# All low halves of the streamed weights on VectorE in a two-layer mixer, none on GpSimd in attention and first merge

## The chip, the cores and the metric

The kernel runs on one core of a Trainium2 chip. The core has TensorE (PE in the profile: matmuls, with its weight loads as PEld), VectorE (DVE), ScalarE (ACT), GpSimd (POOL) and SyncE (SP, which here issues the DMAs). The metric is the device time of one execution in microseconds; less is better.

## The reference, cut to what matters

Two layers over 512 latent tokens and 256 context tokens of 1024 channels, in fp32. Each layer is a mixer of three branches with sigmoid gates, then an MLP with a squared ReLU. The context goes through the same weights; in the last layer only its keys and values are needed.

```python
for l in range(DEPTH):                                     # 2
    mod, mod_c = c_act @ w_ada[l] + b_ada[l], cc_act @ w_ada[l] + b_ada[l]
    h = modulate(rms_norm(x, norm1[l]), sh1, sc1)          # hc from xc in the same way
    (u, qs, ks_, vs, q1, q2, k1, k2, vd, gl) = project_streams(h @ w_in[l], ...)
    y_pool = pool_mixer(u, w_pool[l], pool_scale[l])
    y_swa = windowed_gqa_latent(qs, ks_, vs, ksc, vsc, swa_sink[l])
    y_diff = diff_head_out(diff_attention_latent(q1, q2, k1, k2, vd, ...), ...)
    merged = (g[..., 0, :] * (y_pool @ w_br_pool[l]) + g[..., 1, :] * (y_swa @ w_br_swa[l])
              + g[..., 2, :] * (y_diff @ w_br_diff[l]))    # g = sigmoid(gl)
    x = x + g1 * (merged @ w_out[l])
    h2 = modulate(rms_norm(x, norm2[l]), sh2, sc2)
    x = x + g2 * (jnp.square(jax.nn.relu(h2 @ w_ff1[l])) @ w_ff2[l])
    # layer 0: the same for the context xc
return x
```

## The kernel before

**Products in three parts.** Every fp32 operand of a large product is held as a high half H, its rounding to the matmul's fp32r type, and a low half L = operand - H. A product is hi*hi + hi*lo + lo*hi, three matmuls into one PSUM tile (L229 to L231 in `unit`, L376 in the projections, L988 to L990 in the gates).

**The stream of weights.** All weights of both layers lie in memory as one stream of tiles of 128 rows and up to 768 columns, in the order of their use. `dma_tile` loads the next tile into one of three raw buffers; all these loads are issued by SyncE in the order of the stream. `split_tile` takes the next raw tile, calls `split` and lets the next load go. `split` (L168) issues two instructions, both recorded at their own lines: ScalarE's copy to the high half (L170) and the subtraction that gives the low half (L171), on the engine `eng`, or on VectorE where `eng` is None. The result is a W tile, of which six exist (RING). `ensure` splits up to a given tile; `blocks` asks for the tiles of a unit and for some ahead of them.

**Who takes the low halves.** The tiles of the MLP and of the windowed groups are subtracted on VectorE. On GpSimd are those of the four differential groups (`group`), of the gates beside attention (`gate_filler`), of the gates and branches of the first layer's merge (the tables WG and WB, one entry for a layer), of half of the output projection (OUTE) and of some tiles of the prologue and of the first layer's MLP (PW, FE). Other work of GpSimd: the reciprocal roots (L178), a part of the rotary embedding (L439) and of its gains (L409, L413), halves of the y of two branches (YP, also L171, but with `y` as its output), and a part of the modulated activations h.

**The stages**, in us of the profiled execution: the prologue (to 60: first norm and modulation, first products); the first layer's attention (60 to 584: two windowed groups, four differential ones, where the projection of the next group and gates fill in between the softmax steps; the last part has the pooling branch as filler); the merge (584 to about 755: remaining gates, 24 branch products, each gated on VectorE at L1294 and L1298 and summed at L1301; beside it the modulation columns of later stages, dot products of VectorE with DMA'd rows of w_ada, L259); the output projection and the MLP (to 1340). The second layer repeats this from 1340 with less context work: attention 1400 to 1750, merge and output to 1925, MLP to the end.

**What sets the order.** Each engine works through its instructions in the order of the program. A list scheduler orders them by when their inputs are expected and by priorities (the table PRI, and `high_priority` ahead of L1294 and L1298); in the prologue the order is the one that is written. A split is thus placed where the scheduler thinks that its copy is done.

**Names**: W_nnn a W tile; E the exponentials of a softmax and PT their transposes (L702, L777, L592 scale E; L542, L719 take the low half of PT from PSUM); ob the output of attention, scaled; d, nm, rt, rc small columns of the softmax; x, xn, h activations and gs a gain; mg the merged branches, tgl a reloaded gate, br a branch product; junk the output of the dot products L259, of which only the sum counts.

Of the kernel before, what the change touches and what calls it, by code (L numbers as in the profile page):

```python
# [13 lines left out]
PSUM = bass.MemoryType.PSUM  # L14
# [13 lines left out]

# gates of the first branches that are worked out beside the attention of each group
GATES_AT = ((5, 5, 3, 3, 0, 1), (5, 5, 3, 3, 3, 1))  # L30
# [5 lines left out]
def unit_plan(l):  # L36
    """Each layer's weights in the order of their use: (name, index, tiles of 128 rows)."""
    g = START[l]
    seq = [("swa", 0, 0)] + [("gate", j, 8) for j in range(g)]
    for i, n in enumerate(GATES_AT[l]):  # L40
        if i < 5:
            seq.append(("swa", 1, 0) if i == 0 else ("diff", i - 1, 0))
        seq += [("gate", g + j, 8) for j in range(n)]
        g += n
    tail = [x for x in seq if x[0] == "gate"][g - GATES_AT[l][5]:]
    seq = [x for x in seq if x not in tail]
    seq += [("u", m, 8) for m in range(4)] + [("wp", 0, 4)] + tail
    seq += [(name, i, 8 if name == "gate" else 4) for name, i in merge_plan(l)]
    seq += [("out", m, 8) for m in range(8)] * 2
    return seq + [(name, i, 8 if name == "ff1" else 4) for name, i, _, _ in mlp_plan(l)]  # L50


def merge_plan(l):
    """Gates that are left after the attention, and the branches."""
    g = (START[l] + sum(GATES_AT[l]))
    first = min(24, max(g, 16) + AHEAD)
    seq = [("gate", i) for i in range(g, first)]
    for i in range(24):
        if i >= 16 and first < 24:
            seq.append(("gate", first))  # L60
            first += 1
        seq.append(("br", i))
    return seq


def mlp_plan(l):
    """The MLP by parts of 512 hidden channels: (name, unit, part, turn), the first units of a part before the
    second product of the last one. The last part of the first layer goes over the latents and then the context."""
    parts = [(e, 0) for e in range(8)] + ([(7, 1)] if l == 0 else [])
# [11 lines left out]
def stream_plan(seq):  # L81
    """Columns of each tile of the stream, and where each unit's row tiles lie in it."""
    tiles, where, room = [], {}, 0
# [31 lines left out]
MGP = ()  # L115
WG = ("pool", None)
WB = (("pool", "pool"), (None, None))
ATT = {"Q": 5, "E": 4, "PT": 3, "y": 2, "ph": 2, "zs": 3, "st": 6}
# [15 lines left out]
class Kern:  # L134
# [6 lines left out]

# [1 line left out]
    def T(self, name="T", dtype=F32):  # L143
# [17 lines left out]
    def psum(self, name, g, s):  # L161
        """The pool of the phase that begins: g single banks and s pairs of them."""
        if self.ps is not None:
# [9 lines left out]
    def rsqrt(self, out, in_, n, scale):  # L173
        """out = (in_*scale + eps) ** -0.5"""
        nc = self.nc
        t = self.sm(n, "ms")
        nc.vector.tensor_scalar(t, in_, scale, EPS, ALU.mult, ALU.add)  # L177
        nc.gpsimd.tensor_tensor(out, t, self.mhalf[:, 0:n], op=ALU.pow)  # L178

# [1 line left out]
    def dma_tile(self):  # L181
# [10 lines left out]
    def split_tile(self, eng=None):  # L192
        """Split the next tile of the weight stream into its two parts."""
        if self.pos >= len(TILES):
# [17 lines left out]
    def blocks(self, l, name, idx, ahead=2, eng=None, turn=0):  # L212
        """The row tiles of a unit's weights as (tile, column) pairs."""
        w = [(FIRST[l] + i, o) for i, o in STREAMS[l][1][name, idx][turn]]
        self.ensure(w[-1][0] + ahead, eng)
        return [(self.loaded[i], o) for i, o in w]

# [1 line left out]
    def unit(self, ps, W, acts, groups, off=0):  # L219
        """ps[:, tokens] = sum_k W_k^T acts_k as hi*hi + hi*lo + lo*hi."""  # L220
        mm = self.nc.tensor.matmul
# [10 lines left out]

# [1 line left out]
    def silu2(self, out, c, t):  # L234
        """2 * silu(c)"""
        self.nc.scalar.activation(t, c, AF.Tanh, scale=0.5)
# [18 lines left out]
    def ada_dot(self, pool, w, c, l, j):  # L255
        """Modulation column j as a product of rows; c holds twice the vector."""
        for v in range(2 if l == 0 or j < 16 else 1):
# [5 lines left out]
    def ada(self, raw, js):  # L263
        """Modulation columns, one of 128 channels at a time; the last layer's context needs only a norm."""
        pool, c = self.cvec(raw)
# [12 lines left out]

# [1 line left out]
    def norm_stats(self, x, a, b):  # L280
        """The tokens' 1/rms on every partition, in PSUM."""
        nc = self.nc
# [21 lines left out]
    def gains(self, l, v, j0, norm0):  # L304
        """gain * (1 + scale), for a norm whose scale starts at modulation column j0."""
        gs = self.cp.tile([128, 8], F32, name=f"gs{l}_{v}_{j0}")
# [9 lines left out]
    def modulate(self, t, h, k, a, b, gs, sh):  # L316
        """h = t * gain + shift in two parts; t is overwritten."""
        nc = self.nc
# [5 lines left out]
    def norm_apply(self, x, a, b):  # L324
        """x / rms in place."""
        bc = self.norm_stats(x, a, b)
# [12 lines left out]

# [1 line left out]
    def group(self, l, kind, gi):  # L341
# [3 lines left out]
        else:  # L345
            d = self.group_w(l, kind, gi, self.nc.gpsimd if kind == "diff" else None)
        if d["swa"]:
# [9 lines left out]
    def group_w(self, l, kind, gi, eng):  # L357
        """The weights and the shape of a group."""
        return dict(kind=kind, gi=gi, Q={}, swa=kind == "swa", dims=(4, 1, 64) if kind == "swa" else (2, 2, 128), done=set(),
                    W=[t for t, _ in self.blocks(l, kind, gi, 0, eng)])  # L360

    def proj_mm(self, l, h, d, t, k0, k1):
        """Half of the projection of token tile t."""
        st = d.setdefault(t, {})
# [127 lines left out]

# [1 line left out]
    def diff_unit(self, l, d, qt):  # L494
# [76 lines left out]
    def diff_ctx(self, l, d):  # L571
        """The two context query tiles of one head, over the context keys."""
        nc = self.nc
# [73 lines left out]

# [1 line left out]
    def swa_unit(self, l, d, qt, hp):  # L649
# [90 lines left out]
    def swa_ctx(self, l, d, qt):  # L740
        """One context query tile of four heads, over the context keys."""
        nc = self.nc
# [66 lines left out]

# [1 line left out]
    def attention(self, l, h, tail):  # L811
# [81 lines left out]
    def gate_filler(self, l, h, first, last):  # L893
        """Gates in half units, kept in memory until the merge."""
        nc = self.nc
        for i in range(first, last):
            W = self.blocks(l, "gate", i, 0, nc.gpsimd)
            for (a, b) in ((0, 384), (384, 768)) if l == 0 else ((0, 256), (256, 512)):
# [8 lines left out]

# [1 line left out]
    def kv(self, shape, name, dtype=F32):  # L909
        return self.kp.tile(shape, dtype, tag="KV", name=name)  # L910

    def pool_branch(self, l, h, groups):
        """u, the pooled means and their mixing; in steps, beside other work."""
        nc = self.nc
# [86 lines left out]

# [1 line left out]
    def prologue(self, pl):  # L1003
        """The first layer's norm, modulation and first products, in the order that is written here."""
        nc, a = self.nc, self.a
# [143 lines left out]
    def small(self, rows, P):  # L1149
        """Sinks, gains, lambdas and the scale of the heads' outputs."""  # L1150
        nc = self.nc
# [19 lines left out]

# [1 line left out]
    def run(self):  # L1173
# [48 lines left out]
        for l in range(DEPTH):  # L1222
# [12 lines left out]

            # attention
            if l > 0:
# [13 lines left out]

            # branches and merge
            pb = tc.tile_pool(name=f"pb{l}", bufs=1, reuse_waits="tile")
# [59 lines left out]

            # output projection, residual, MLP
            pm = tc.tile_pool(name=f"pm{l}", bufs=1, reuse_waits="tile")
# [111 lines left out]
def host_arrays(inp):  # L1427
# [59 lines left out]
    rows = np.concatenate(rows + [np.zeros(3 * 512 - DEPTH * ROWS_L, np.float32)]).reshape(3, 512)  # L1487
    # constants of the shapes alone
    f32 = np.float32
# [45 lines left out]
```

## Time and profile before

| | us |
|---|---|
| median of three runs (lowest to highest) | 2308.11 (2307.55 to 2310.36) |
| span of the profiled execution | 2309.9 |
| TensorE busy | 2212.6 (96%) |
| VectorE busy | 1502.7 (65%) |
| ScalarE busy | 962.3 (42%) |
| GpSimd busy | 520.8 (23%) |

The page gives the busy time of each engine; TensorE's share says how much of the span could go at most without fewer or faster matmuls. The stretches (windows) give the same by stage. A group of instructions of one line shows their count, mean duration and what the engine waited for ahead of them; the view of one line gives the least, median and greatest duration, which tells whether an instruction always takes the same time. The timeline lists single instructions with start and duration, and in brackets how long the engine stood idle ahead of one and for whom. The list of TensorE's waits sums these brackets.

### The profile page before, as it was taken

The numbers are of one execution on the slowest core, as the hardware profiler recorded it, in microseconds if no ns is written. First come the engines' busy times: TensorE is split into PE (matmuls) and PEld (weight loads), VectorE is DVE, ScalarE is ACT, GpSimd is POOL, SyncE is SP. The second block draws the span as 40 slices with busy tenths as digits, with TensorE's granted clock in tenths as the row PEclk, the third lists the DMA queues.
The fourth block names the chain that finished last, engine by engine and source line by source line (L and its number), as shares of the span: only waits on it lengthen the run. The fifth ranks groups of instructions, "written<-read, shape, count | busy, mean of one in ns | idle before, by whom it ended". The sixth has DMA issues, their size and how long they took to land.

```text
span 2309.9 us, 34112 instructions
## 1 busy us (share of the span) xinstructions
PE 2212.6 (96%) x12924; PEld 1969.0 (85%) x12924; DVE 1502.7 (65%) x2757; ACT 962.3 (42%) x1979; POOL 520.8 (23%) x525
## 2 busy tenths in 40 slices
PE   7999999989988999999999989999999999999999
PEld 2999999988876888888888879999998788888887
DVE  6667676777799776655555487766668577544443
ACT  4466655565212442222222244655556435332331
POOL 4334245432442200000000033434551122000000
PEclk9999999999998999999999989999999999999999
DMA  6222122212774543333333342212222654333332
GB/s 256 84 56 79 53 74 77 68 36 84 254 255 152 188 121 126 121 129 124 127 125 105 89 132 70 75 56 83 74 74 82 203 186 130 105 95 96 94 96 76
DMA packets 108668, 260.53 MB, mean 113 GB/s; under 512 B 13012, under 2 KB 33620, under 8 KB 107223
## 3 DMA queue, kind: packets, MB, share of 16 engines
q1 hardware_dynamic: 108502, 258.35, 35.2%
q8 instruction: 102, 1.67, 0.3%
q14 instruction: 64, 0.52, 0.1%
HBM read 233.00 MB, written 25.30 MB: 112 GB/s over the span
## 4 chain that ended last, share of the span: by engine, by line
PE 47%; issue 26%; DVE 15%; DMA 4%; ACT 4%; POOL 3%; SPq 0%; POOLq 0%; DVEq 0%; ACTq 0%
PE z L376 7%; PE ff L231 5%; PE ff L230 5%; PE ff L229 5%; PE gate L988 3%; PE gate L990 3%; PE gate L989 3%; DMA raw<-in_w_dram 2%; DMA wada<-in_wada_dram 2%; POOL W L171 2%; DVE junk L259 2%; DVE W L171 1%; ACT W L170 1%; PE ptr L715 1%; PE ada L1047 1%
## 5 line engine op out<-in xcount | busy, mean ns | idle before, releaser
L170 ACT ACTIVATE W<-raw 128x768 fp32r<-128x768 f32 (+1 forms) x383 | 320.2, 838 | 576.7 <-PE ff L231 428.2
L171 DVE TENSOR_TENSOR W<-raw,W 128x768 fp32r<-128x768 f32 x243 | 236.4, 974 | 189.4 <-ACT W L170 183.5
L376 PE MATMUL z<-W,h 128*128 128x384 f32 (+2 forms) x1728 | 313.5, 332 | 10.5 <-POOL h L1077 4.3
L171 POOL TENSOR_TENSOR W<-raw,W 128x768 fp32r<-128x768 f32 (+1 forms) x140 | 267.7, 1920 | 203.2 <-ACT W L170 199.3
L376 PEld LDWEIGHTS z<-W,h 128*128 128x128 f32 x1728 | 286.8, 191 | 14.6 <-POOL h L1077 5.1
L229 PE MATMUL ff<-h,W 128*128 128x512 f32 (+1 forms) x800 | 280.6, 351 | 1.2 <-ACT r L1350 1.2
L230 PE MATMUL ff<-h,W 128*128 128x512 f32 (+1 forms) x800 | 280.8, 351 | 0.0
L231 PE MATMUL ff<-h,W 128*128 128x512 f32 (+1 forms) x800 | 280.1, 350 | 0.0
L178 POOL TENSOR_TENSOR rs<-ms,mhalf 128x4 f32<-128x4 f32 (+4 forms) x79 | 79.7, 1009 | 867.2 <-DVE ms L177 829.0
L230 PE MATMUL ff<-f,W 128*128 128x512 f32 x736 | 264.2, 359 | 0.1
L229 PE MATMUL ff<-f,W 128*128 128x512 f32 x736 | 263.2, 358 | 0.0
L231 PE MATMUL ff<-f,W 128*128 128x512 f32 x736 | 262.4, 357 | 0.0
L259 DVE CUSTOM_DVE_ANT_0 junk<-wada,cbc,cols 128x1024 bf16<-128x1024 f32 x128 | 188.1, 1469 | 55.2 <-DMA wada<-in_wada_dram 54.4
L988 PE MATMUL gate<-h,W 128*128 128x256 f32 (+1 forms) x656 | 215.3, 328 | 6.4 <-DVE ob L554 6.4
L989 PE MATMUL gate<-h,W 128*128 128x256 f32 (+1 forms) x656 | 215.6, 329 | 0.0
L990 PE MATMUL gate<-h,W 128*128 128x256 f32 (+1 forms) x656 | 212.4, 324 | 0.0
L1380 DVE SCALAR_TENSOR_TENSOR x<-ff,mod,x 128x512 f32<-128x512 f32 (+1 forms) x192 | 121.4, 657 | 105.0 <-PE ff L231 104.8
L229 PEld LDWEIGHTS ff<-h,W 128*128 128x128 f32 x800 | 151.3, 189 | 22.9 <-ACT r L1350 1.4
L231 PEld LDWEIGHTS ff<-h,W 128*128 128x128 f32 x800 | 151.1, 189 | 21.6
L230 PEld LDWEIGHTS ff<-h,W 128*128 128x128 f32 x800 | 151.2, 189 | 21.4
L229 PEld LDWEIGHTS ff<-f,W 128*128 128x128 f32 x736 | 138.7, 189 | 21.7
L231 PEld LDWEIGHTS ff<-f,W 128*128 128x128 f32 x736 | 138.3, 188 | 21.3
(263 smaller groups left out, 4721.6 us busy)
## 6 DMA issues: line engine op xcount, KB each, us to landing
raw<-in_w_dram SPq DMA_DIRECT2D x375, 384.0 KB, 3.1
wada<-in_wada_dram SPq DMA_DIRECT2D x80, 512.0 KB, 4.1
wa<-in_wada_dram SPq DMA_DIRECT2D x8, 1024.0 KB, 8.1
tgd<-tgs SPq DMA_DIRECT2D x38, 192.0 KB, 2.3
tgl<-tgd SPq DMA_DIRECT2D x19, 384.0 KB, 4.5
tgd<-tgs SPq DMA_DIRECT2D x44, 128.0 KB, 1.9
tgl<-tgd SPq DMA_DIRECT2D x22, 256.0 KB, 4.2
yl<-yd SPq DMA_DIRECT2D x12, 384.0 KB, 3.9
```

The lines of the kernel that those rows point to most:

```text
L170: nc.scalar.activation(H, src, AF.Copy)
L171: (eng or nc.vector).tensor_tensor(L, src, H.bitcast(F32), op=ALU.subtract)
L178: nc.gpsimd.tensor_tensor(out, t, self.mhalf[:, 0:n], op=ALU.pow)
L229: mm(ps[:, a:b], wh, x[0][:, r], start=k == 0, stop=False)
L230: mm(ps[:, a:b], wh, x[1][:, r], start=False, stop=False)
L231: self.last_mm = mm(ps[:, a:b], wl, x[0][:, r], start=False, stop=k == nk - 1)
L259: self.nc.vector.tensor_tensor_reduce(junk, w, c[:, v, :], 0.5, self.col(l, 21 + j), ALU.mult, ALU.add, self.mod[l][:, v, j:j + 1])
L376: self.nc.tensor.matmul(z[:, c0:384], h[k][:, hpart, ts], d["W"][k // 2][:, wpart, (k % 2) * 384 + c0:(k % 2 + 1) * 384], start=(k == 0 an ...
L988: mm(ps, wh, x[:, 0, a:b], start=k == 0, stop=False)
L989: mm(ps, wh, x[:, 1, a:b], start=False, stop=False)
L990: return mm(ps, wl, x[:, 0, a:b], start=False, stop=k == len(acts) - 1)
L1380: nc.vector.scalar_tensor_tensor(x[m][:, ga:gb], ps[:, ga:gb], self.mod[l][:, v, 40 + m:41 + m], x[m][:, ga:gb], ALU.mult, ALU.add)
```

## The change

Four arguments change; each named GpSimd for a low half of W and now names none, which means VectorE. ScalarE's copies, the loads and their order, the ring and all numbers stay. (The other lines of the full diff only blank comments.)

```diff
@@ tables of the module
-WG = ("pool", None)
-WB = (("pool", "pool"), (None, None))
+WG = (None, None)
+WB = ((None, None), (None, None))
@@ group
-            d = self.group_w(l, kind, gi, self.nc.gpsimd if kind == "diff" else None)
+            d = self.group_w(l, kind, gi, None)
@@ gate_filler
-            W = self.blocks(l, "gate", i, 0, nc.gpsimd)
+            W = self.blocks(l, "gate", i, 0, None)
```

`blocks` also splits the tiles ahead of a unit on the engine named for it, so at the borders a tile of a neighbouring unit moves too. In the built program GpSimd has 140 subtractions of W before and 30 after, VectorE 243 and 353.

GpSimd, end of the prologue. x, h: the parts of the first activations that GpSimd modulates, the numbers 169 and 170 two of their buffers.

```order
 L171 TENSOR_TENSOR W_396<-raw,W_396 128x768
 L171 TENSOR_TENSOR W_401<-raw,W_401 128x768
-L171 TENSOR_TENSOR W_579<-raw,W_579 128x768
 L1074 TENSOR_SCALAR x_3_157<-x_3_157,gs_1_8_172,mod_124 128x256
 L1077 TENSOR_TENSOR h_169<-x_3_157,h_169 128x256
 L1074 TENSOR_SCALAR x_3_157<-x_3_157,gs_1_8_172,mod_124 128x256
 L1077 TENSOR_TENSOR h_170<-x_3_157,h_170 128x256
-L171 TENSOR_TENSOR W_584<-raw,W_584 128x768
```

Two splits are gone from GpSimd; the first stood ahead of the last two tiles of h, the second behind them. In VectorE's row they stand ahead of gs and behind its last h.

VectorE, first layer's attention, at about 185 to 190 us: the softmax of one query tile of a windowed group, whose scaled E (L702) TensorE transposes next.

```order
 L678 ISA nm 128x1
 L686 TENSOR_TENSOR d<-nm,nsink 128x2
+L171 TENSOR_TENSOR W_2243<-raw,W_2243 128x768
 L693 TENSOR_TENSOR rt<-r,es 128x2
 L695 RECIPROCAL rc<-rt 128x2
 L702 TENSOR_SCALAR E<-E,rc 128x512
+L171 TENSOR_TENSOR W_2248<-raw,W_2248 128x768
 L434 TENSOR_TENSOR xn<-zs,rg 128x320
 L732 TENSOR_TENSOR y<-O,ob 64x256
```

Two splits came into the row: one between the softmax's columns d and rt, one behind L702.

VectorE, the merge of the first layer: dot products of the modulation beside the gated branches.

```order
 L259 ISA junk,mod_124<-wada,cbc,cols 128x1024
 L259 ISA mod_124 128x1
+L171 TENSOR_TENSOR W_7205<-raw,W_7205 128x768
+L171 TENSOR_TENSOR W_7280<-raw,W_7280 128x768
 L1294 SCALAR_TENSOR_TENSOR mg<-tgl,br 128x768
 L259 ISA junk,mod_124<-wada,cbc,cols 128x1024
```

Two splits came in ahead of the first gated branch (L1294); the dot products keep their places around it.

## Rows read from the trace of the kernel before

**Rows 1.** The page, part 1: busy us, share of the span, instructions.

```profile
PE 2212.6 (96%) x12924; PEld 1969.0 (85%) x12924; DVE 1502.7 (65%) x2757; ACT 962.3 (42%) x1979; POOL 520.8 (23%) x525
```

**Rows 2.** Stretches: window, length, busy us of each engine (instructions), PEclk, DMA share, GB/s.

```profile
60.00:460.00 400.00, 390.62 (x2459) 380.36 (x2459) 267.20 (x646) 229.20 (x588) 152.42 (x165) 0.99 0.24 69
622.00:715.00 93.00, 80.30 (x434) 68.78 (x433) 90.40 (x109) 15.72 (x19) 32.66 (x15) 0.96 0.69 234
```

**Rows 3.** Groups, GpSimd, 60 to 460 us: busy us, mean ns, idle before.

```profile
L171 POOL TENSOR_TENSOR W<-raw,W 128x768 fp32r<-128x768 f32 x37 | 70.4, 1910 | 23.5 <-ACT W L170 23.4
```

**Rows 4.** Line L171, W: min/median/max ns, first and last start, forms.

```profile
L171 DVE TENSOR_TENSOR W<-raw,W x243: 694/958/2181, 89.3 to 2283.3; 128x768 fp32r<-128x768 f32 x121, 128x512 fp32r<-128x512 f32 x1
...
L171 POOL TENSOR_TENSOR W<-raw,W x140: 919/1846/2844, 38.0 to 1911.8; 128x768 fp32r<-128x768 f32 x133, 128x512 fp32r<-128x512 f32 x6, 128x256 fp32r<-128x256 f32 x1
```

**Rows 5.** Four other lines of VectorE, the same columns.

```profile
L702 DVE TENSOR_SCALAR E<-E,rc x32: 486/553/2052, 126.3 to 1578.4; 128x512 f32<-128x512 f32 x16, 128x640 f32<-128x640 f32 x16
L719 DVE TENSOR_TENSOR PT<-ptr,PT x80: 408/691/693, 130.7 to 1585.0; 128x512 fp32r<-128x512 f32 x64, 128x256 fp32r<-128x256 f32 x16
L259 DVE CUSTOM_DVE_ANT_0 junk<-wada,cbc,cols x128: 1271/1284/2926, 589.5 to 1244.6; 128x1024 bf16<-128x1024 f32 x128
L1301 DVE TENSOR_TENSOR mg<-mg,tgl x25: 677/947/2597, 663.1 to 1887.6; 128x512 f32<-128x512 f32 x14, 128x768 f32<-128x768 f32 x11
```

**Rows 6.** Timeline, first layer's attention: start us, us, engine, line.

```profile
187.51 1.84 POOL L171 TENSOR_TENSOR W<-raw,W 128x768 fp32r<-128x768 f32 x1
...
187.80 1.83 DVE L702 TENSOR_SCALAR E<-E,rc 128x512 f32<-128x512 f32 x1
```

**Rows 7.** Timeline, first layer's merge.

```profile
639.64 1.93 POOL L171 TENSOR_TENSOR W<-raw,W 128x768 fp32r<-128x768 f32 x1 [2.16 <-ACT W L170]
639.93 2.72 DVE L259 CUSTOM_DVE_ANT_0 junk<-wada,cbc,cols 128x1024 bf16<-128x1024 f32 x1
```

**Rows 8.** Groups by form, VectorE and GpSimd, merge, 584 to 715 us.

```profile
L259 DVE CUSTOM_DVE_ANT_0 junk<-wada,cbc,cols 128x1024 bf16<-128x1024 f32 x47 | 80.2, 1706 | 5.7 <-DMA wada<-in_wada_dram 5.1
L1301 DVE TENSOR_TENSOR mg<-mg,tgl 128x768 f32<-128x768 f32 x9 | 15.1, 1680 | 0.0
L171 POOL TENSOR_TENSOR W<-raw,W 128x768 fp32r<-128x768 f32 x18 | 41.5, 2308 | 52.8 <-ACT W L170 52.8
L171 POOL TENSOR_TENSOR y<-yl,y 128x768 fp32r<-128x768 f32 x6 | 13.3, 2217 | 25.5 <-ACT y L170 19.0 <-DMA wada<-in_wada_dram 6.5
```

**Rows 9.** What TensorE waits for, 60 to 460 us: total us, times, longest.

```profile
PE tr L473 <- DVE d L763: 2.2, 1, 2.2
PE ptr L715 <- DVE E L702: 1.4, 2, 0.7
PE tr L473 <- ACT E L592: 1.4, 1, 1.4
```

**Rows 10.** The same, second layer's attention, 1400 to 1750 us.

```profile
PE gate L988 <- DVE ob L554: 3.7, 2, 1.8
PE ptr L715 <- DVE E L702: 2.4, 2, 1.5
...
PE O L550 <- DVE PT L542: 1.4, 2, 0.8
```

**Rows 11.** The same, merge, 584 to 715 us.

```profile
PE br L229 <- DVE mg L1294: 6.2, 2, 3.3
```

**Rows 12.** Timeline, end of the prologue.

```profile
49.59 5.56 POOL L171 TENSOR_TENSOR W<-raw,W 128x768 fp32r<-128x768 f32 x3
...
57.59 2.68 PE L376 MATMUL z<-W,h 128*128 128x384 f32 x6 [4.31 <-POOL h L1077]
```

**Rows 13.** Timeline, start of the second layer.

```profile
1370.78 2.54 POOL L171 TENSOR_TENSOR W<-raw,W 128x768 fp32r<-128x768 f32 x1
...
1371.96 2.18 DVE L171 TENSOR_TENSOR W<-raw,W 128x768 fp32r<-128x768 f32 x1
...
1374.19 1.65 PE L376 MATMUL z<-W,h 128*128 128x384 f32 x4 [1.17 <-DVE W L171]
```

## What the change will do to the time: the prediction

> **What bounds the kernel now.** I read the share of each engine first. The reader should see that TensorE is busy 96% of the span and that nothing else is near: VectorE 65%, GpSimd 23% [rows 1]. A change on VectorE and GpSimd can therefore only take away, or add to, the few microseconds in which TensorE stands still. Next the stretches: in the long stretch of the first layer's attention (60 to 460 us) VectorE is busy 267 of 400 us, in the merge it is busy 90.4 of 93 us, which is 97% [rows 2]. So attention has room on VectorE and the merge has none. Then the two forms of the instruction that moves: a 128x768 low half has a median of 0.958 us on VectorE and 1.846 us on GpSimd [rows 4].
>
> The view that decides is the spread of the other VectorE instructions. L702 takes 0.486 us at best and 2.052 at worst, L259 1.271 and 2.926, L1301 0.677 and 2.597, while L719, which reads PSUM, never exceeds 0.693 [rows 5]. The timeline shows what the long ones have in common. An L702 starts at 187.80 and ends at 189.63; a GpSimd split started at 187.51 and ended at 189.35 [rows 6]. An L259 starts at 639.93 and takes 2.72; a GpSimd split ran until 641.57, and 641.57 plus an undisturbed 1.28 is 642.85, about where the L259 ends [rows 7]. I read this as: a VectorE instruction with its inputs in SBUF stands still until the GpSimd split that began before it is through. So the splits on GpSimd are not free for VectorE, and the question is whether VectorE loses more by doing them or by waiting for them.
>
> **What moves.** The order of the built program shows 110 splits gone from GpSimd's row (140 before, 30 after) and 110 more in VectorE's (243, then 353). By place: 2 in the prologue, 45 in the first layer's attention, 18 in its merge, 2 at the second layer's start, 43 in its attention. Six are of 512 columns at 0.694, 104 of 768 at 0.958: 6 x 0.694 + 104 x 0.958 = 103.8 us of new VectorE work. GpSimd loses some 205 us (110 x about 1.87; in the long stretch 37 of them were 70.4 us [rows 3]). None of this is on TensorE by itself: in the list of what TensorE waits for there is hardly a W outside the second layer's start, since the ring of six W tiles keeps them ready before use. That a single split becomes 0.9 us shorter is therefore costed at nothing; the ring hides it. What counts is what happens to VectorE's other instructions, stage by stage.
>
> **Merge of the first layer (584 to 715 us).** Removed: the standing still. 47 L259 at a mean of 1.706 against 1.284 undisturbed are 19.8 us too long, 9 L1301 at 1.680 against 0.947 are 6.6 us too long [rows 5, 8], 26.4 together. GpSimd ran 41.5 us of W splits and 13.3 us of y splits, which stay [rows 8]; the share of W is 41.5 / 54.8 = 76%, so 20.0 us go. Added: 18 x 0.958 = 17.2 us. Net on VectorE: -2.8. As VectorE is full there, and TensorE waits for its mg (6.2 us in two waits [rows 11]), the net goes to the end nearly whole. I take **-3**, with bounds of 0 (TensorE's waits have another cause) and -5 (the y halves that run beside are freed too).
>
> **Attention of both layers.** Added: 45 and 43 splits, 88 in all: about 41 us of VectorE work in each layer. Removed: held instructions. Pairing each VectorE instruction of two SBUF inputs (or one tensor_scalar) that exceeds its usual time with the split running beside it gives about 30 us a layer. Net some +10 us of VectorE work a layer in stretches with 130 us of free time, so throughput there is not the matter; single waits of TensorE are. From the lists of waits [rows 9, 10]:
> - E L702, 1.4 + 2.4 = 3.8 us in four waits. Each follows a held L702, as at 187.80. The hold was about 1.3 us, longer than the 0.7 waited there. I take -3.3.
> - d L763, 2.2 us. Two GpSimd splits stand beside the VectorE chain that leads to it. The splits come onto VectorE as 2 x 0.96, less than the 2 holds. I take -1.7.
> - E L592 1.4, PT L542 1.4, ob L554 3.7: 6.5 us where the held instruction stands further up the chain. I take a little under half, -2.9.
>
> Together **-7.9**; bounds 0 (each time the next wait comes up) and about -11.
>
> **Second layer's start.** A VectorE split of W took 2.18 us because a GpSimd split from 1370.78 to 1373.32 held it, and TensorE waited 1.17 us for it [rows 13]. With both on VectorE, the second stands behind the first, so the first takes 0.96: 2.18 - 0.96 = 1.22 us. **-1.2**.
>
> **Prologue.** GpSimd ran three W splits from 49.59 to 55.15, and TensorE then waited 4.31 us for GpSimd's h [rows 12]. The third of these goes to VectorE, so GpSimd's x and h start a third of 5.56, some 1.9 us, earlier. On VectorE it costs 0.96 ahead of gs, which delays ScalarE's part, but that part is done long before GpSimd's. **-1.9**; bounds 0 and -1.9.
>
> **Allowance.** 88 splits now stand in VectorE's row ahead of instructions that TensorE may wait for. When a copy by ScalarE ends late, VectorE's row stops. I allow **+2** (bounds 0 and +8).
>
> Sum: -3 - 7.9 - 1.2 - 1.9 + 2 = **-12**. The profiled execution's span is 2309.9, 1.8 above the median of the runs, 2308.1; from the span I get 2297.9, and with the same distance between the two **2296** for the median.
>
> **The rivals.**
> 1. *The waits only change their name.* TensorE's waits in attention are short and each has a next one close behind; if nothing of the 7.9 comes and half of the rest, the gain is about 3 us: 2305. For it: TensorE idles only about 9 of 400 us in the long stretch. Against it: the gains of merge and prologue don't rest on that.
> 2. *VectorE's row stops for ScalarE's copy: slower.* A split needs ScalarE's copy of the same tile, which waits for the tile's DMA. GpSimd's 37 splits of the long stretch waited 23.4 us for that copy, 0.63 us each [rows 3]. On GpSimd this hurt nobody; on VectorE the softmax of the group stands behind it. If two splits at each of the 12 starts of groups make TensorE wait, it costs 12 x 2 x 0.63 = 15 us, and the attention's -7.9 is lost: 2308 - 6 + 15 = 2317. It decides from 0.14 us of TensorE's time per moved split (88 x 0.14 = 12 eats the gain). Against it: the order puts each split where its copy is planned to be done.
> 3. *The merge is the bound: slower.* If the long L259 came from the traffic of the DMAs and not from GpSimd, VectorE would get 17.2 us more in a stretch that is 97% full and nothing back: 2308 + 17.2 - 7.9 - 1.2 - 1.9 + 2 = 2316. It decides once less than 17.2 - 9.0 = 8.2 of the 26.4 us goes, a third. Against it: L259 of 1.28 us and of 2.7 us stand side by side in the same traffic.
> The Trainium skill ("Perfetto Trace Analysis", section "Optimizing Scalar/DVE Operations") says that where DVE is saturated, giving some work to ScalarE or GpSimd may make sense; this change does the contrary in a saturated stretch, and by that rule alone the rival of 2316 would win. The same section adds that DVE and GpSimd share a read port of SBUF, so that moving work between those two might not help, and the held L259 agrees with the second sentence rather than the first (2.72 against 1.28 us).
> 4. *More goes than I counted.* If all that the splits hold turns into shorter chains (the 400 - 390.6 = 9.4 us that TensorE stands still in the long stretch [rows 2], as much in the second layer's attention, the merge's 6.2 and the 3.1 of the two starts), the gain is near 28: 2280.
> 5. *The change doesn't do what it says*: excluded by the order of the built program, which shows the 110 moved.
>
> **How the numbers follow.** Forecast (2289 to 2303) 0.67; more 0.05; waits change their name 0.15; slower by the row of VectorE 0.07; slower by the merge 0.06. About 0.2% (4.6 us) is what a measurement of this kernel can tell from no change, so faster means under 2303.5: 0.67 + 0.05 = 0.72; same 0.15; slower 0.13. The range leaves out the slower cases and most of the larger gain: 2284 to 2309.
>
> **What would show it.** If the steps are right: GpSimd's busy time falls by about 205 us and VectorE's grows by about 20 (103.8 added, 20 of holds in the merge and some 60 in the attentions removed); in 622 to 715 the mean L259 falls from 1.706 to about 1.35, not to 1.284, as y splits remain; L702 keeps near 0.5; the waits on E L702 and d L763 are gone; TensorE's wait for h in the prologue falls from 4.31 to about 2.4. If L259 stays at 1.7, rival 3 holds and the step on standing still is wrong. If TensorE has new waits whose releaser is a PT, E or Q of VectorE with a W split just ahead in its row, rival 2 holds. If VectorE grows by 100 us, the holds had another cause.

## The result and the profile after

The changed kernel takes 2275.2 us (median of four runs, 2274.2 to 2276.4) against 2308.5 before: a ratio of 0.986 with a 95% interval of 0.9848 to 0.9872, 33 us faster. The forecast was 2296 with a range of 2284 to 2309: the sign came out right, the forecast gain of 12 is about a third of what came, and the time lies below the range.

The page of the changed kernel, part 1 (busy us, share, instructions; it answers to [rows 1]), and the stretches that answer to [rows 2], with the second layer's attention, whose row in the kernel before stands in the third block (window, length, busy us of PE, PEld, DVE, ACT, POOL, granted clock, DMA share, GB/s):

```profile
PE 2202.3 (97%) x12924; PEld 1963.7 (86%) x12924; DVE 1517.3 (67%) x2867; ACT 963.5 (42%) x1979; POOL 324.9 (14%) x415
```
```profile
60.00:446.00 386.00, 385.18 (x2454) 376.57 (x2454) 272.29 (x683) 228.96 (x586) 84.98 (x125) 1.00 0.23 72
608.00:691.00 83.00, 78.65 (x438) 68.29 (x437) 80.36 (x111) 15.92 (x20) 7.18 (x3) 0.98 0.74 255
...
1373.00:1714.00 341.00, 338.17 (x2564) 333.49 (x2563) 249.05 (x628) 205.78 (x522) 81.99 (x134) 1.00 0.24 75
```
```profile
1400.00:1750.00 350.00, 340.25 (x2565) 333.44 (x2564) 239.66 (x583) 204.69 (x522) 154.90 (x177) 1.00 0.25 73
```

VectorE took over 110 splits and grew by 1517.3 - 1502.7 = 14.6 us, not by the 103.8 of their own time: the rest came back from instructions that no longer stand still. GpSimd lost 196 us. In the long stretch of the first attention TensorE stood still 400 - 390.6 = 9.4 us before and 386 - 385.2 = 0.8 after, and its busy time for nearly the same matmuls fell by 5.4 as well. In the second layer's attention it was 9.8 before and 2.8 after.

The durations, line by line (min/median/max in ns, first and last start), which answer to [rows 5], and the groups of the merge, which answer to [rows 8]:

```profile
L702 DVE TENSOR_SCALAR E<-E,rc x32: 471/517/555, 123.7 to 1547.1; 128x512 f32<-128x512 f32 x16, 128x640 f32<-128x640 f32 x16
L259 DVE CUSTOM_DVE_ANT_0 junk<-wada,cbc,cols x128: 1269/1280/2871, 574.6 to 1220.3; 128x1024 bf16<-128x1024 f32 x128
```
```profile
L259 DVE CUSTOM_DVE_ANT_0 junk<-wada,cbc,cols 128x1024 bf16<-128x1024 f32 x45 | 60.9, 1352 | 5.9 <-DMA wada<-in_wada_dram 5.6
L171 DVE TENSOR_TENSOR W<-raw,W 128x768 fp32r<-128x768 f32 x17 | 19.4, 1146 | 0.0
L1301 DVE TENSOR_TENSOR mg<-mg,tgl 128x768 f32<-128x768 f32 x10 | 9.5, 954 | 0.0
...
L171 DVE TENSOR_TENSOR y<-yl,y 128x768 fp32r<-128x768 f32 x6 | 7.3, 1225 | 0.0
```

L702 never exceeds 0.555 us now (2.052 before). L259 still reaches 2.87, beside the y splits and the output projection's W splits that stay on GpSimd. What TensorE waits for in the long stretch, in the merge, and in the second layer's attention (answers to [rows 9 to 11]; total us, times, longest):

```profile
PE tr L473 <- DVE rot L462: 0.7, 1, 0.7
PE z L376 <- ACT zs L395: 0.2, 1, 0.2
```
```profile
PE br L230 <- DVE y L171: 4.3, 1, 4.3
```
```profile
PE gate L988 <- DVE ob L554: 1.3, 2, 0.6
PE ptr L715 <- DVE Q L489: 0.8, 1, 0.8
```

The waits on E, d, PT and mg that the forecast had named are all gone, and most of ob. To see where the time went I laid the two traces side by side: each TensorE instruction of the one against the same of the other, and the difference of their starts at the borders of the stages.

| stage (us of before) | forecast | by the two traces |
|---|---|---|
| prologue, to 95 | -1.9 | +0.3 |
| first attention, 95 to 584 | some -3.6 | -13.7 |
| merge and output, 584 to 820 | -3 | -10 |
| MLP, and start of the second layer to 1400 | -1.2 | -3.5 |
| second attention, 1400 to 1750 | some -4.3 | -8.9 |
| the rest | 0 | -1.7 |
| allowance | +2 | |
| sum | -12 | -37.4 |

The sum of the traces is their spans' difference, 2309.9 - 2272.5; the span of the profiled execution lies 2.7 us below the median time for the changed kernel and 1.4 above it for the one before, which leaves 33 for the medians.

### The profile page after: what moved, and what is told of

Read it like the earlier page. It is cut to its first block, busy times and chain, and to the rows that moved or that the text cites. A ratio compares the mean times of both kernels' runs of the same rounds, so it can differ in the third digit from the quotient of the medians.

```text
span 2272.5 us, 34132 instructions
## 1 busy us (share of the span) xinstructions
PE 2202.3 (97%) x12924; PEld 1963.7 (86%) x12924; DVE 1517.3 (67%) x2867; ACT 963.5 (42%) x1979; POOL 324.9 (14%) x415
## 4 chain that ended last, share of the span: by engine, by line
PE 50%; issue 26%; DVE 14%; DMA 4%; ACT 3%; POOL 2%; SPq 0%; DVEq 0%; ACTq 0%; POOLq 0%
PE z L376 9%; PE ff L231 5%; PE ff L230 5%; PE ff L229 5%; PE gate L988 4%; PE gate L989 4%; PE gate L990 4%; DVE junk L259 2%; DVE W L171 2%; DMA raw<-in_w_dram 2%; PE ptr L715 1%; DVE nm L513 1%; DMA wada<-in_wada_dram 1%; PE ada L1047 1%; PE br L230 1%
## 5 line engine op out<-in xcount | busy, mean ns | idle before, releaser
L171 DVE TENSOR_TENSOR W<-raw,W 128x768 fp32r<-128x768 f32 (+1 forms) x353 | 346.8, 984 | 224.0 <-ACT W L170 219.6
L259 DVE CUSTOM_DVE_ANT_0 junk<-wada,cbc,cols 128x1024 bf16<-128x1024 f32 x128 | 173.9, 1359 | 52.1 <-DMA wada<-in_wada_dram 51.6
L229 PEld LDWEIGHTS ff<-f,W 128*128 128x128 f32 x736 | 138.8, 189 | 21.7
L231 PEld LDWEIGHTS ff<-f,W 128*128 128x128 f32 x736 | 138.3, 188 | 21.3
L230 PEld LDWEIGHTS ff<-f,W 128*128 128x128 f32 x736 | 138.6, 188 | 20.8 <-DVE f L1353 0.5
```

The lines of the kernel that those rows point to most:

```text
L171: (eng or nc.vector).tensor_tensor(L, src, H.bitcast(F32), op=ALU.subtract)
L229: mm(ps[:, a:b], wh, x[0][:, r], start=k == 0, stop=False)
L230: mm(ps[:, a:b], wh, x[1][:, r], start=False, stop=False)
L231: self.last_mm = mm(ps[:, a:b], wl, x[0][:, r], start=False, stop=k == nk - 1)
L259: self.nc.vector.tensor_tensor_reduce(junk, w, c[:, v, :], 0.5, self.col(l, 21 + j), ALU.mult, ALU.add, self.mod[l][:, v, j:j + 1])
```

## The experiments

**Each stage alone.** e1 has the two edits in attention, e2 the two tables of the merge.

```diff
 e1 (against the changed kernel)
-WG = (None, None)
-WB = ((None, None), (None, None))
+WG = ("pool", None)
+WB = (("pool", "pool"), (None, None))
```

> The two edits in attention alone; the merge's W stay on GpSimd. In the trace of the whole change TensorE's instructions of the first layer's attention come 14 us earlier, of the second layer's start 3, of its attention 10. If each stage's gain is its own (GpSimd's splits hold VectorE there), this kernel gains 25 to 28 us: about 2282. If the stages hang together (the merge needs what attention leaves), it gains clearly less than 25 or more than 28. If the attention's gain comes from the prologue's two tiles, the shift is there already at 60 us.

> The two tables of the merge alone; attention stays as before. By its own stage's gain in the trace it gains about 10 us: 2298. By the prediction's term (VectorE's work less the holds) it gains 3: 2305. If VectorE's extra 17 us counted, it would be slower, 2316.

Measured: e1 2286.2, ratio 0.9908 [0.9893, 0.9922], 22 us faster; e2 2298.4, 0.9953 [0.9939, 0.9968], 10 us faster, against 2308.4. The two parts add up to 32, the change's 33: the stages' gains are their own. Groups of the whole program, e1 and then e2 (busy us, mean ns, idle before):

```profile
L259 DVE CUSTOM_DVE_ANT_0 junk<-wada,cbc,cols 128x1024 bf16<-128x1024 f32 x128 | 186.5, 1457 | 45.9 <-DMA wada<-in_wada_dram 45.1
...
L702 DVE TENSOR_SCALAR E<-E,rc 128x512 f32<-128x512 f32 x16 | 7.8, 485 | 0.4
```
```profile
L259 DVE CUSTOM_DVE_ANT_0 junk<-wada,cbc,cols 128x1024 bf16<-128x1024 f32 x128 | 174.8, 1366 | 44.9 <-DMA wada<-in_wada_dram 44.1
...
L702 DVE TENSOR_SCALAR E<-E,rc 128x512 f32<-128x512 f32 x16 | 16.2, 1013 | 0.6
```

The attention's L702 is undisturbed (485 ns) exactly where the attention's splits are gone, and the merge's L259 falls exactly where the merge's are. e1's 22 is less than the 25 to 28 expected from one pair of traces; it has the prologue and the start of the second layer in it as well.

**Is it the holding?** e3 and e4 leave everything as in the changed kernel and give GpSimd idle work at the places of the moved splits.

```diff
 e3, in split, for the moved tiles
+            nc.gpsimd.tensor_tensor(self.shadow[:, 0:H.shape[-1]], H.bitcast(F32), H.bitcast(F32), op=ALU.subtract)
 e4, in its place
+            for _ in range(3):
+                m = nc.gpsimd.memset(self.shadow[:, 0:H.shape[-1]], 0.0)
 ...                                # m waits for ScalarE's copy to H
```

> As the changed kernel, all low halves on VectorE, and for each of the 110 moved splits GpSimd subtracts the high half from itself into a spare tile that nobody reads. VectorE's work, the loads and the time at which a W is ready are those of the changed kernel; GpSimd is as busy as before and reads SBUF. If GpSimd's reading instructions hold VectorE, the gain is gone and VectorE's new 104 us come on top: 2305 to 2330, and L702 is again up to 2 us long. If the gain came from W tiles being ready earlier or from another order, about 2275 to 2280.

> As the one before, but GpSimd fills the spare tile three times with zeros in place of the subtraction, after the same copy of ScalarE: busy at the same places, reading nothing. If only GpSimd's reading holds VectorE's two-input instructions, L259 and L1301 keep their undisturbed 1.28 and 0.95 us and the time is 2275 to 2285. If any GpSimd work holds VectorE, or if the gain came from GpSimd having more time for its own small chains (reciprocal roots, rotary embedding), it is 2295 or more. L702, with one input in SBUF, tells the two kinds of VectorE instructions apart.

Measured: e3 2334.8, ratio 1.0115 [1.0097, 1.0133], 26 us slower than before and 5 above what was expected; e4 2285.6, 0.9903 [0.9886, 0.992], at the upper end of the 2275 to 2285 for reading alone. The page's part 1 and the lines of GpSimd's idle work and of L702 (in e3 at L705, in e4 at L708), e3 and then e4; for e4 also the least, median and greatest duration of L702 and of the scaling of ob (L568, in the other kernels L562):

```profile
PE 2219.5 (95%) x12924; PEld 1974.3 (84%) x12924; DVE 1600.8 (68%) x2867; ACT 961.6 (41%) x1979; POOL 522.0 (22%) x525
```
```profile
L705 DVE TENSOR_SCALAR E<-E,rc 128x512 f32<-128x512 f32 x16 | 13.2, 825 | 0.4
...
L174 POOL TENSOR_TENSOR shadow<-W 128x768 bf16<-128x768 f32 x104 | 192.5, 1851 | 137.2 <-ACT W L170 122.4 <-DVE tgl L1302 8.4 <-DMA tgl<-tgd 4.6
```
```profile
PE 2200.0 (97%) x12924; PEld 1961.4 (86%) x12924; DVE 1518.0 (67%) x2867; ACT 961.5 (42%) x1979; POOL 562.2 (25%) x745
```
```profile
L708 DVE TENSOR_SCALAR E<-E,rc 128x512 f32<-128x512 f32 x16 | 9.1, 567 | 0.4
...
L175 POOL MEMSET shadow<- 128x768 bf16 x312 | 231.2, 741 | 116.4 <-ACT W L170 103.6
```
```profile
L708 DVE TENSOR_SCALAR E<-E,rc x32: 469/553/870, 124.3 to 1547.2; 128x512 f32<-128x512 f32 x16, 128x640 f32<-128x640 f32 x16
...
L568 DVE TENSOR_SCALAR ob<-ob,rso x32: 271/286/732, 338.8 to 1769.8; 128x128 f32<-128x128 f32 x32
```

This is the decisive pair. With the same VectorE instructions in both, VectorE's busy time is 1600.8 us beside GpSimd instructions that read SBUF and 1518.0 beside longer ones (231 against 193 us) that only write: 83 us of standing still, against 1517.3 in the changed kernel. So it is GpSimd's reading instructions that hold VectorE, and not the order, which in e3 is that of the changed kernel on VectorE, ScalarE and SyncE instruction by instruction. VectorE's busy time is the measure here rather than e3's time: in e3 GpSimd also keeps some W tiles longer, and ScalarE's copies waited 6.6 us for that.

The zeros are not quite without effect. In e4 VectorE's tensor_scalar instructions (one input tile in SBUF and a column as a factor) still stand still at times: L702 takes up to 0.870 us (0.555 in the changed kernel) and the scaling of ob up to 0.732 (0.290). The long ones ran beside a filling, and ob's ended with it (a filling from 1618.42 to 1619.15, ob from 1618.50 to 1619.23). The instructions with both inputs in SBUF kept their times beside a filling, and so did L259 (1.28).

e4 is some 10 us slower than the changed kernel (ratios 0.9903 and 0.986). By the two traces it is 3 us slower in the first attention and 5 in the second, and 4 faster in the merge and output. GpSimd's row is there as full as before, so its small chains, which attention needs (reciprocal roots, the rotary embedding), can come later. So about two thirds of the 33 us are the reading alone; up to a third is GpSimd's row having become free, together with what the zeros hold. Up to, because e4's idle work is longer than the splits were; no run separates the two. I had not counted this part at all.

**What a wait costs.** e5 is the kernel before, with transposes of the unit matrix put into two of TensorE's waits.

```diff
         tr = self.g("tr")
+        self.warm(tr, {5: 20, 23: 13}.get(self.n_tr, 0))   # n_tr counts the calls of proj_tr
 ...                                # warm puts them behind the last matmul of z (L376)
```

> The kernel before, with 20 and 13 extra transposes of the unit matrix on TensorE, put into its two waits at 101.2 to 103.7 us and 380.7 to 382.2 us (their results are overwritten). Nothing else changes. If the half clock (0.50) that follows such waits comes from TensorE's standing still, the granted clock after 103.7 stays at 1.00, TensorE is 1.6 us earlier from there on, and after 382.2 up to 1.6 us: 2305 to 2306 in all. If the clock falls for another reason, the shift is 0 and the time 2308.

The stretches of 2 us around the first wait, before and then e5 (columns as above):

```profile
102.00:104.00 2.00, 0.34 (x3) 0.37 (x4) 1.59 (x5) 0.59 (x3) 0.00 (x0) 0.96 0.74 233
104.00:106.00 2.00, 2.00 (x8) 2.00 (x7) 0.47 (x3) 2.00 (x10) 0.01 (x1) 0.50 0.04 15
106.00:108.00 2.00, 2.00 (x9) 2.00 (x9) 2.00 (x6) 0.96 (x4) 1.13 (x1) 0.68 0.02 4
```
```profile
102.00:104.00 2.00, 2.00 (x21) 2.00 (x20) 1.68 (x5) 0.50 (x3) 0.00 (x0) 1.00 0.66 197
104.00:106.00 2.00, 2.00 (x16) 2.00 (x14) 0.38 (x3) 1.97 (x10) 0.00 (x0) 1.00 0.01 5
106.00:108.00 2.00, 2.00 (x14) 1.91 (x13) 2.00 (x6) 0.71 (x3) 1.14 (x1) 1.00 0.02 4
```

Before, TensorE stood still for 2.2 us, and then ran at 0.50 of its clock (1.2 of 2.4 GHz) and did 8 and 9 matmuls where e5, which was kept busy, did 16 and 14. TensorE is 1.8 us earlier from there on and another 1.8 after the second place, where 1.6 and up to 1.6 were expected. In the whole it doesn't show: 2307.3 against 2307.2, ratio 1.0001 [0.9991, 1.001]; in the trace half of the 4.8 us that are gained at 460 us is given back later, and the rest is within the interval. The 2305 to 2306 that were expected did not come. So the local cost of a wait is shown (2.2 us of standing still and 1.8 more), that it reaches the end is not.

**Why the merge gained 10.** In the merge before, SyncE stood 4.5 us in three waits for GpSimd's split to free a raw buffer, with the reloads of the gates (tgl, for which L1294 waits) behind it in its queue; e9 to e14 test whether that is the reason.

```profile
SPq L188 <- POOL W L171: 4.5, 3, 2.4
```

```diff
 e9 (against before), e10 (against the changed kernel)
-RAW = 3
+RAW = 4
-            B = _Tagged(raw, {"tg": 8, "mg": 8})
+            B = _Tagged(raw, {"tg": 7, "mg": 8})
 e11 (against before)
-                nc.sync.dma_start(t[:, 0:n], self.tgd[i][:, 0:n])
+                nc.scalar.dma_start(t[:, 0:n], self.tgd[i][:, 0:n])
```

> The kernel before with four raw buffers for the loads of W in place of three (and seven gate buffers in place of eight, for the room). In the merge before, SyncE's next load of W stood 2.4 us for a raw buffer that GpSimd's split still read, and behind it the reloads of the gates (tgl), for which VectorE's first L1294 and then TensorE waited. If this queue is what made the merge's gain larger than VectorE's balance, a fourth raw buffer takes the stop away without moving a split: the first L1294 lands 2 to 4 us earlier, 3 to 6 us less in the merge, 2302 to 2305. If VectorE's own row is the bound there, nothing changes, 2307 to 2308.

> The changed kernel with four raw buffers (and seven gate buffers). By the queue: the merge's part of the gain is partly had by the buffer, so the step from the kernel with four raw buffers to this one is 27 to 30 us, less than the 33 of the change. By VectorE's row: the step stays 33, and this kernel is at 2274 to 2275.

> The kernel before with the reloads of the gates (tgl, 27 loads in both merges) issued from ScalarE's queue in place of SyncE's, so that they don't stand behind the loads of W. By the queue: the first L1294 starts 3 us or more earlier, 2300 to 2305. By VectorE's row: 2307 to 2308. If ScalarE's copies are late for it: slower, 2310 or more.

Measured: e9 2309.0, ratio 1.0004 [0.9993, 1.0014]; e10 2278.4, 0.9881 [0.9862, 0.99], 30.5 below e9; e11 2311.5, 1.0021 [1.0013, 1.003]. Neither the buffer nor the other queue gains by itself. e10 decides nothing either: its 30.5 lies between the 27 to 30 of the queue and the 33 of VectorE's row, and its six runs scatter from 2274.9 to 2288.7. e9 was 5 us earlier than before until 700 us and lost this again in a wait of 6.3 us for y. e13 and e14 ask directly: the merge alone on VectorE, GpSimd filling a spare tile with zeros, and in e14 GpSimd then reading 8 columns of the raw tile, meant to keep its buffer taken as long as before.

```diff
 e13, e14, in split, for the 24 tiles of the merge
+            for _ in range(3):
+                m = nc.gpsimd.memset(self.shadow[:, 0:H.shape[-1]], 0.0)
 ...                                # m waits for ScalarE's copy to H
 e14 alone
+            nc.gpsimd.tensor_tensor(self.shadow[:, 0:8], src[:, 0:8], src[:, 0:8], op=ALU.subtract)
```

> The merge alone on VectorE (2298.4), and GpSimd fills a spare tile with zeros three times (about 2.2 us) after ScalarE's copy of each of the 24 tiles: GpSimd busy as before, nothing read, raw buffers free as early as without. Either theory: 2297 to 2300. It is the control for the next.

> As the one before, and after the three fillings GpSimd reads 8 columns of the raw tile, so that the raw buffer stays taken as long as by GpSimd's split before, while no long GpSimd instruction reads SBUF beside VectorE. If the late raw buffer made the merge's larger gain, SyncE's loads and the gates' reloads come late again and 4 to 8 us are lost: 2302 to 2306. If the held instructions alone made it, 2297 to 2300, and L259 stays at 1.3 us.

Measured: e13 2297.8, ratio 0.9954 [0.994, 0.9968]; e14 2298.4, 0.9947 [0.9929, 0.9965]; both as e2 (2298.4). SyncE's waits for GpSimd and L259 in e14's merge:

```profile
SPq L195 <- POOL shadow L178: 7.6, 2, 4.0
```
```profile
L266 DVE CUSTOM_DVE_ANT_0 junk<-wada,cbc,cols 128x1024 bf16<-128x1024 f32 x49 | 71.4, 1458 | 9.7 <-DMA wada<-in_wada_dram 9.4
```

The first branch product and the first reloads of a gate, before and then e14; and what SyncE waits for with its loads of W in the merge of the changed kernel:

```profile
605.85 0.39 PE L229 MATMUL br<-y,W 128*128 128x512 f32 x1
612.80 1.45 SPq L1273 DMA_DIRECT2D tgl<-tgd  x2
```
```profile
601.35 0.39 PE L236 MATMUL br<-y,W 128*128 128x512 f32 x1
605.38 0.90 SPq L1281 DMA_DIRECT2D tgl<-tgd  x2
```
```profile
SPq L188 <- DVE W L171: 19.0, 11, 4.6
```

SyncE stands 7.6 us for GpSimd in e14, more than before, and the gain of 10 us stays. But all of the 7.6 lies before 600 us, ahead of the first branch product. The first reload goes out 4.0 us behind that product, as in e13 (4.0) and e2 (4.3), and not 6.9 us behind it as before. So e14 did not bring back the late reload that it was made to test, and e9 had not taken it away (6.6). What e13 and e14 do show is that the gain stays when GpSimd is kept busy without the splits.

The late reload can hardly be the whole of the gain: the first gated branch (L1294) starts 11.8 us behind the first product before and 7.9 in e2, which is 4 us of the 10, and in the changed kernel SyncE stands longer for raw buffers than before (19.0 against 4.5 us), now for VectorE's splits. Whether it has a part stays open. L259 did not stay at 1.3 us in e14 (1.458), since y splits and the first splits of the output remain on GpSimd in that window.

**Going on.** e6 to e8 take more splits from GpSimd: the output projections (e6), y too (e7), the prologue's and the MLP's too (e8). e12 is e7 with the gates' reloads on ScalarE's queue.

```diff
-OUTE = ("pool", None)
+OUTE = (None, None)      # e6
-YP = (1, 3)
+YP = ()                  # e7
-FE = "pool"
+FE = None                # e8
-PW = "pool"
+PW = None                # e8
```

> The changed kernel, and the 20 W tiles of the output projections that GpSimd still splits go to VectorE too. If holding is the whole matter, the waits on mh and x there shrink as in the attention: 2 to 6 us less than the changed kernel, 2270 to 2273. If VectorE is the bound there (92% busy in 692 to 796 us) the added 19 us show, and TensorE waits longer for W: 2278 or more.

> As the one before, and the halves of y that GpSimd splits go to VectorE too, so that GpSimd does no split in merge and output. By holding: the y splits of GpSimd run 2.3 us, VectorE's cost 0.95, so L259 falls to 1.28 throughout and another 2 to 4 us go: 2267 to 2271. By VectorE being full in the merge: no change against the one before, or 2 us more.

> As the one before, and the splits of the prologue (5 tiles) and of the end of the first layer's MLP (6): GpSimd splits nothing any more. In the changed kernel's prologue gs (L312) took 1.83 in place of 0.64 us since GpSimd's remaining split held it, and TensorE waited 2.9 us for what follows; by holding this goes, 2 to 3 us at 60 us. If VectorE is late in the prologue with 5 more splits, TensorE waits there for W or h and 1 to 4 us are lost.

> The kernel with GpSimd's splits of merge, output and y on VectorE as well (2266.8), with the gates' reloads on ScalarE's queue. By the queue: 2 to 5 us less in the merges, 2262 to 2265. If VectorE is the bound in the merge: 2266 to 2268.

Measured: e6 2272.1, ratio 0.9852 [0.9836, 0.9868]; e7 2266.8, 0.9829 [0.9812, 0.9845]; e8 2266.7, 0.9827 [0.9812, 0.9841]; e12 2274.6, 0.985 [0.9834, 0.9865]. e6 can't be told from the change itself (0.986); e7 and e8 are below its interval, by 0.3%, and can't be told from each other. In e6 the waits for mh and x shrink as expected, but TensorE then waits 6.3 us for one copy by ScalarE of a W at the start of the output projection (7.4 in e7). L259 in e7's merge (570 to 690 us) and the page of e8, part 1:

```profile
L259 DVE CUSTOM_DVE_ANT_0 junk<-wada,cbc,cols 128x1024 bf16<-128x1024 f32 x45 | 57.7, 1281 | 6.0 <-DMA wada<-in_wada_dram 5.9
```
```profile
PE 2198.1 (97%) x12924; PEld 1961.2 (87%) x12924; DVE 1513.4 (67%) x2907; ACT 963.9 (43%) x1979; POOL 250.3 (11%) x375
```

With the y splits gone L259 is at its undisturbed 1.281 throughout, as expected. e8's VectorE does 40 instructions more than the changed kernel's and is busy 3.9 us less. Two W splits are still on GpSimd in e8, in the prologue (at 38.9 and 44.3 us), where none was expected. The 2 to 3 us that were expected at 60 us came and went: TensorE's waits for h there fell from 4.1 us in e7 to 1.9, and the next wait, for rot (L450), rose from 0.3 to 2.9.

The reloads on ScalarE's queue cost some 5 us (e12 against e7 by their ratios, whose intervals overlap) where 2 to 5 were hoped for as a gain; e11's ratio shows a loss too. The traces show where: a reload that waits for a free gate buffer now stands in ScalarE's queue, and ScalarE's copies of W stand behind it. In e12's merge:

```profile
ACT W L170 <- DVE mg L1294: 22.7, 2, 13.0
```

Neither e7 nor the kernel before has such a wait in the merge.

## Why the prediction was wrong in size, by its steps

**That GpSimd's splits hold VectorE: right.** It was the step on which all rested; L702's maximum fell from 2.05 to 0.56 us, VectorE grew by 14.6 us where about 20 was said, and e3 against e4 shows the cause. The trace of before had the answer to the rival of the DMAs' traffic too: of its 128 L259, 18 took 2.0 to 2.9 us, each of them beside a GpSimd split, and the other 110 took at most 1.287.

**Attention, -7.9 forecast, -22.6 by the traces (22 in e1, which has the prologue and the second layer's start in it as well): the failed step.** It was mis-sized: the forecast priced single waits of TensorE, some at half and each at its own length. In the long stretch [rows 2] and in the second attention TensorE's standing still alone fell by 8.6 + 7.0 = 15.6 us, and its busy time by 5.4 + 2.1 = 7.5. Three things were missing. First, for the waits whose held instruction stands further up the chain I took a little under half; all but ob's 1.3 us went. The list of the long stretch also had waits on ob that the sum left out, and they went too:

```profile
PE ptr L610 <- DVE ob L554: 2.2, 1, 2.2
...
PE gate L988 <- DVE ob L554: 1.1, 1, 1.1
```

Second, a wait was costed at its own length. TensorE's busy time in the long stretch fell by 5.4 us for nearly the same matmuls, beside the 8.6 us of waits, and over the whole program by 10.3 (2212.6 to 2202.3) for the same 12924: behind some of the waits it had run at half clock, as at 104 us (e5 shows it there). In the second attention the clock is 1.00 in both, and there the busy time fell by 2.1 only. Third, a GpSimd that is free sooner: e4 is 3 and 5 us slower than the changed kernel in the two attentions, which bounds this and does not show its parts.

**Merge, -3 forecast, -10 measured (e2): mis-sized.** The holds that went are (1.706 - 1.352) x 47 = 16.6 for L259, (1.680 - 0.954) x 9 = 6.5 for L1301, (1.446 - 1.225) x 6 = 1.3 for y (its mean before was 1.446 us), together 24.4 where 20.0 was said for the first two; the share of W in the holds was larger than its share in GpSimd's time. The 17 splits of VectorE took 19.4 us where 17.2 were said, some of them held by the y splits in turn. The balance is -5.0, the bound that I had named, though for another reason: the y splits stayed. The step that failed is that the net of VectorE's row would be the stage's gain. TensorE's own list of the merge before has more waits beside the 6.2 us for mg [rows 11]:

```profile
PE br L230 <- DVE y L171: 4.6, 2, 3.2
PE br L229 <- DVE tgl L1298: 1.9, 2, 1.3
```

Together they are 12.7 us, of which 4.3 are left: 8.4 of the 10. The two waits for mg were not spread over the stage but stood behind two held L259, one of them that at 639.93 [rows 7]. Some 2 us more are clock (0.96 before in 622 to 715 [rows 2], 0.98 after in 608 to 691). Whether the late reload of the gates has a part in these waits, e9 to e14 leave open.

**Prologue, -1.9 forecast, nothing measured: wrong, and the reason stands in the rows.** The new order, in the trace of after:

```profile
49.90 4.32 POOL L171 TENSOR_TENSOR W<-raw,W 128x768 fp32r<-128x768 f32 x2
...
51.07 1.49 DVE L171 TENSOR_TENSOR W<-raw,W 128x768 fp32r<-128x768 f32 x1
...
52.48 1.83 DVE L312 SCALAR_TENSOR_TENSOR gs<-mod,cols 128x2 f32<-128x2 f32 x2
54.27 2.50 ACT L1072 ACTIVATE h<-x,mod,gs 128x512 fp32r<-128x512 f32 x4 [4.29 <-DVE gs L312]
...
55.63 0.62 PE L376 MATMUL z<-W,h 128*128 128x384 f32 x2 [2.87 <-ACT h L1072]
...
57.66 2.61 PE L376 MATMUL z<-W,h 128*128 128x384 f32 x7 [1.41 <-POOL h L1077]
```

The split that came onto VectorE cost 1.49 us, not 0.96, and pushed gs behind the start of GpSimd's next split, which runs until 54.22 and held gs until then. ScalarE's h, which I called done long before, became the late one: 2.87 + 1.41 = 4.28 us of waits in place of 4.31 [rows 12]. I had applied the holding to what goes away and not to what stays.

**Second layer's start, -1.2 forecast, -3.0 from 1340 to 1400: right in kind.** The second wait for W (1.17 us [rows 13]) is gone; TensorE's busy time fell as well, from 46.7 to 44.2 us for the same 293 matmuls, at a granted clock of 0.86 before (1340 to 1400) and 0.94 after (1316 to 1373):

```profile
1344.61 1.85 DVE L171 TENSOR_TENSOR W<-raw,W 128x768 fp32r<-128x768 f32 x1
...
1346.52 2.24 PE L376 MATMUL z<-W,h 128*128 128x384 f32 x10 [1.46 <-DVE W L171]
1346.78 0.94 DVE L171 TENSOR_TENSOR W<-raw,W 128x768 fp32r<-128x768 f32 x1
```

**The allowance of +2 and the two slower rivals: not seen.** No wait on a W of VectorE came up in the attentions, and L259 fell, so neither VectorE's row (2317) nor the merge as a bound (2316) decided. The Trainium skill ("Perfetto Trace Analysis", section "Optimizing Scalar/DVE Operations") says that giving a saturated VectorE's work to GpSimd may make sense; here, in a stretch that was 97% busy [rows 2], the move back gained 10 us (e2). Its caution in the same section, that such a move might not help as the two share a read port, agrees with that. The fourth rival, all of these waits going at once (2280), came nearest, and got a chance of 0.05; the result lies 5 us below even that, since it too counted waits alone.

## What to carry to other kernels

Where VectorE's instructions with SBUF inputs have a maximum far above their median, look for GpSimd instructions that were running when they began; work moved from GpSimd to VectorE can then cost VectorE almost nothing, and the list of what the slow engine waits for is better taken whole than by halves. When you apply such a rule, apply it also to the GpSimd instructions that stay, and to the new place of what moves. And where the granted clock falls behind a wait of TensorE, cost the wait with the matmuls that follow at half clock; e5 shows this on the spot, and also that taking away two such waits alone need not reach the end.

## What the runs showed of the hardware that I had not expected

- GpSimd filling a 128x768 tile with zeros (0.74 us each, 231 us in all) left VectorE's busy time at 1518.0 us, against 1517.3 without; GpSimd subtracting (193 us in all) raised it to 1600.8. Beside the zeros it was nearly always a tensor_scalar instruction of VectorE that stood still: L702 up to 0.870 us against 0.555, the scaling of ob up to 0.732 against 0.290.
- After a wait of 2.2 us at 104 us TensorE ran at a granted clock of 0.50 for some 3 us; with transposes put into the wait it stayed at 1.00.
